# A mixer trunk's three gated merges taken in another order, and a list scheduler that models the port VectorE and GpSimd share

## The chip, the cores and the metric

The kernel runs on one core of a Trainium2 chip. The metric is the device time of one launch in microseconds; a kernel's time is the median of its runs. The engines are called by the profile's names: PE is TensorE's matmul side, DVE is VectorE, ACT is ScalarE, POOL is GpSimd, SP issues the DMAs.

## The reference, cut to what matters

Two layers of a mixer with three parallel branches. Each branch gives a 1024 x 512 result, each result goes through its own projection to 1024 columns, is weighted by a sigmoid gate, and the sum of the three goes through an output projection and is added to the stream.

```python
for l in range(DEPTH):                                   # DEPTH = 2
    h = _rmsnorm(x, norm_g[l])
    (... , gate_logits) = _split_cols(h @ w_in[l])
    y_a = _spatial_gating(...)                           # first branch
    y_b = _mla(...)                                      # second: attention, 8 heads
    y_c = _gla(...)                                      # third: gated linear attention
    gates = jax.nn.sigmoid(gate_logits + b_gate[l]).reshape(bn, s, N_BRANCH, d)
    merged = (gates[:, :, 0] * (y_a @ w_branch[l, 0])
              + gates[:, :, 1] * (y_b @ w_branch[l, 1])
              + gates[:, :, 2] * (y_c @ w_branch[l, 2]))
    x = x + merged @ w_out[l]
```

## The kernel before

Everything is held transposed (columns on partitions) and the sequence of 1024 is cut into two halves h of 512. Numbers are float32, but matmuls take pairs: `pair` (through `split`) makes of each operand a rounded part by an ACT copy and a rest by a DVE subtraction, and each product is three matmuls.

The program is written as segments. A segment has a main list (large products on PE, in steps of about 12 matmuls of 512 columns, here called chunks) and a side list (attention and the like), and `weave` spreads the side steps evenly over the main ones. All instructions go into a `Recorder`, which gives each a cost and a latency by a formula (lines 78 to 121). `Order` then makes one list per engine: `due` counts back from the written order of PE when each instruction is wanted, and `run` plays time forward and lets each free engine take the ready instruction with the earliest due time, within a window (`TUNE`: 30 us ahead on PE, 14 on DVE, ACT and POOL, 22 on SP). It also counts the 94 SBUF buffers of tag `g`, and keeps 6 free for what is due within 4 us. The chip then runs each engine's list in order. In `run` an instruction of one engine never slows one of another.

The stretch that matters is the last third of each layer. `side_att(u, 1)` is the attention of the second half: per block of keys three matmuls, two exponentials on ACT, and two POOL operations on 128 x 512 (a rest and a running sum) in `qk`; per head the transposes of `head_T` (PE into PSUM, an ACT copy and a DVE rest out of it), the row maxima of `mx` on DVE, `negm`. It is woven into this main list:

- `main_merge(u, 2, "yc", ...)`: third branch, both halves, 16 chunks. For each of 8 column tiles n: load and split one weight tile (a DVE subtraction), and per half 12 matmuls and `pe_b`: a DVE operation that multiplies the gate (SBUF) with the product (PSUM), written to `u["m", h, n]`.
- `main_merge(u, 0, "ya", ...)`: first branch, both halves, 16 chunks; `pe_b` also adds to `m` (two SBUF inputs). Its sixteen y tiles are loaded by `load_y` after chunk 12 of the third branch.
- `main_merge(u, 1, "yb", False, True, (0,))`: second branch, half 0, 8 chunks, the last merge: besides multiply and add, `pe_b` makes the rounded part (ACT) and the rest (DVE, two SBUF inputs) for the output projection.
- `main_out(u, (0,))`: its first 12 chunks; each column tile needs two weight tiles split, two chunks and one DVE addition out of PSUM.

The next segment has the rest of the output projection of half 0, then the second branch and the output projection of half 1. `ya` and `yc` wait in DRAM; `yb` of half 0 (8 tiles) is made by the attention of half 0 in the segment ahead and stays in SBUF.

Of the kernel before, what the change touches and what calls it, by code (L numbers as in the profile page):

```python
# [48 lines left out]

class Op:  # L50
    __slots__ = ("i", "eng", "call", "reads", "writes", "cost", "lat", "pred", "succ", "free", "due", "need", "at",
                 "size", "left", "ready", "table")


class Recorder:
# [16 lines left out]
    def add(self, eng, what, fn, a, k):  # L72
        op = Op()
        op.i, op.eng, op.call = len(self.ops), eng, (fn, a, k)
        isap = lambda v: isinstance(v, bass.AP)
        outs = [v for n, v in k.items() if n in ("out", "accum_out") and isap(v)]
        ins = [v for n, v in k.items() if n not in ("out", "accum_out") and isap(v)]
        if a:
            outs.append(a[0])
        op.writes = [v.tensor for v in outs]  # L80
        op.reads = [v.tensor for v in ins]
        op.pred, op.free, op.table = [], [], None
        count = lambda v: int(np.prod(list(v.shape)[1:]))
        n = max(count(v) for v in outs + ins)
        op.size = 0
        if eng == "tensor":
            n = count(k["out"])
            w = k["lhsT"] if what == "matmul" else k["in_"]
            if what == "transpose":
                op.cost = 0.109  # L90
            elif w.dtype == F32R:
                op.cost = 0.0145 + max(n, 256) / 2410.0
            else:
                op.cost = 0.104 if n == 1 else 0.01 + 4 * max(n, 64) / 2400.0
            op.lat = op.cost + 0.3
        elif eng == "vector":
            op.cost = 0.07 + n / 960.0
            if what == "reciprocal":
                op.cost = 0.05 + n / 150.0
            if what == "tensor_tensor_scan":  # L100
                op.cost = 0.1 + n / 480.0
            op.lat = op.cost + 0.25
        elif eng == "scalar":
            op.cost = 0.13 + n / 1200.0
            op.lat = op.cost + 0.25
            f = k.get("func")
            if f is not None:
                op.table = "ln" if f == AF.Ln else "sin" if f == AF.Sin else "" if f in (AF.Copy, AF.Square, AF.Abs,
                                                                                          AF.Relu) else "exp"
        elif eng == "gpsimd":  # L110
            op.cost = {"memset": 0.3, "affine_select": 2.0}.get(what, 0.9 + n / 2000.0)
            op.lat = op.cost + 0.3
        else:
            op.cost = 0.47
            op.size = count(outs[0]) * int(outs[0].shape[0]) * 4
            op.lat = 2.2
        self.ops.append(op)
        return op


class Order:
# [70 lines left out]
    def run(self):  # L192
# [11 lines left out]
        events, order = [], []  # L204
        g = max(self.tags.values(), key=lambda t: t["bufs"])
        relax = 0

        def fits(op, ahead):
            for n in op.need:
# [8 lines left out]
        while done < len(ops):  # L218
            while ptr < len(pe) and pe[ptr].at is not None:
                ptr += 1  # L220
            v = pe[ptr].due if ptr < len(pe) else 1e9
            moved = False
            for e in engines:
                if free[e] > now + 1e-9:
                    continue
                back, pick = [], None
                h = pool[e]
                while h:
                    d, i = heapq.heappop(h)
                    op = ops[i]  # L230
                    if d - v > TUNE["ahead"][e] * (3 if relax else 1):
                        back.append((d, i))
                        break
                    if op.ready <= now + 1e-9 and fits(op, d - v):
                        pick = op
                        break
                    back.append((d, i))
                    if len(back) > 400:
                        break
                for b in back:  # L240
                    heapq.heappush(h, b)
                if pick is None:
                    continue
                op, moved, relax = pick, True, 0
                cost, lat = op.cost, op.lat
                if op.table and op.table != table:
                    table = op.table
                    cost, lat = cost + 1.3, lat + 1.3
                op.at = now
                order.append(op)  # L250
                done += 1
                free[e] = now + cost
                end = now + lat
                if e == "sync":
                    dma = max(dma, now + 1.5) + op.size / 230e3
                    end = dma + 0.7
                for n in op.need:
                    t = self.tags[self.of[n][0]]
                    t["live"] += 1
                    t["next"] += 1  # L260
                heapq.heappush(events, (end, op.i))
                for s in op.succ:
                    s.left -= 1
                    s.ready = max(s.ready, end if s.eng != e or e == "sync" and s.reads[0].name in
                                  {t.name for t in op.writes} else now)
                    if not s.left:
                        heapq.heappush(pool[s.eng], (s.due, s.i))
                heapq.heappush(events, (free[e], -1))
            if moved:
                continue  # L270
            if not events:
                if relax:
                    raise RuntimeError("no order")
                relax = 1
                for n in pool.values():
                    for d, i in n:
                        if ops[i].ready > now:
                            heapq.heappush(events, (ops[i].ready, -1))
                if events:
                    now = heapq.heappop(events)[0]  # L280
                continue
            now, i = heapq.heappop(events)
            while True:
                if i >= 0:
                    op = ops[i]
                    for n in {t.name for t in op.reads + op.writes}:
                        if n in self.left:
                            self.left[n] -= 1
                            if not self.left[n] and n in self.of:
                                self.tags[self.of[n][0]]["live"] -= 1  # L290
                if not events or events[0][0] > now + 1e-9:
                    break
                _, i = heapq.heappop(events)
# [8 lines left out]
class Builder:  # L302
# [846 lines left out]
    def main_merge(self, u, br, key, first, last, hs=(0, 1)):  # L1149
# [3 lines left out]

        def sgl(n):
            for h in hs:
                t = u["sg", h, n] = self.g()
                self.load(t, u.pop(("sgd", h, br * 8 + n)))

        def pe_b(n, h):
            def f():  # L1160
                nc = self.nc
                ps = box.pop("p")
                t = u.pop(("sg", h, n))
                nc.vector.scalar_tensor_tensor(out=t, in0=t, scalar=1.0, in1=ps, op0=ALU.add, op1=ALU.mult)
                if first:
                    u["m", h, n] = t
                    return
                m = u["m", h, n]
                nc.vector.tensor_tensor(out=m, in0=m, in1=t, op=ALU.add)
                if last:  # L1170
                    hi, lo = self.g(dt=F32R), self.g(dt=F32R)
                    nc.scalar.activation(out=hi, in_=m, func=AF.Copy, scale=0.5)
                    nc.vector.scalar_tensor_tensor(out=lo, in0=m, scalar=0.5, in1=hi.bitcast(F32), op0=ALU.mult,
                                                   op1=ALU.subtract)
                    u["mh", h, n] = (hi, lo)
                    del u["m", h, n]
            return f
# [338 lines left out]
    def build(self):  # L1516
# [22 lines left out]
        for i, u in enumerate(units):  # L1539
# [26 lines left out]
            m = []  # L1566
# [8 lines left out]
            a10, a11 = self.side_att(u, 1)  # L1575
            segs.append((m, a00 + a01, 0.0, 0.97))
            mc = self.main_merge(u, 2, "yc", True, False)
            m = mc[:12] + [(0.0, f) for f in y["ya"]] + mc[12:] + self.main_merge(u, 0, "ya", False, False)
            o0 = self.main_out(u, (0,))
            m += self.main_merge(u, 1, "yb", False, True, (0,)) + o0[:12]  # L1580
            segs.append((m, a10 + a11, 0.0, 0.97))
            m = o0[12:] + self.main_merge(u, 1, "yb", False, True, (1,)) + self.main_out(u, (1,))
            sd = []
            if nxt:
                l2 = nxt["l"]
# [97 lines left out]
```

## Time and profile before

| | us |
|---|---|
| median of 3 runs | 2055.52 |
| lowest, highest | 2050.74, 2056.92 |
| the profiled execution | 2053.61 |
| its span, first to last instruction | 2051.8 |
| PE busy in it | 2009.3 (98%) |
| DVE busy | 1535.5 (75%) |
| ACT busy | 1010.4 (49%) |
| POOL busy | 534.6 (26%) |

The profile is of one execution, and a row's time is counted from the start of its span. PE counts as busy from a matmul's start to its modelled end, and matmuls overlap. All instructions were recorded through one helper and carry its line, L1603, so they are told apart by engine, operation and tile: `mm` is the PSUM tile of a main product, `sc`, `tr` and `av` those of the side work, `g` any SBUF tile of the general pool.

### The profile page before, as it was taken

How to read it: one execution, taken by the hardware profiler on the slowest of the kernel's cores; microseconds unless marked ns; L12 is line 12 of the kernel's file. 1: busy time of each engine (PE TensorE's matmuls, PEld its weight loads, DVE VectorE, ACT ScalarE, POOL GpSimd, SP SyncE). 2: the span in 40 equal slices, each digit the busy share in tenths (PEclk: the TensorE clock that was granted, in tenths of full speed). 3: DMA queues.
4: the chain of work that ended last, by engine and by line, in shares of the span. 5: the costliest groups of instructions: out<-in, count | busy, mean ns of one | idle time of the engine just before them, and what ended most of it. 6: DMA issues, size and time to landing. Idle time of an engine off the chain costs nothing. (4 is left out here: it accounts for less than half of the span.)

```text
span 2051.8 us, 29332 instructions
## 1 busy us (share of the span) xinstructions
PE 2009.3 (98%) x9864; PEld 1650.9 (80%) x9864; DVE 1535.5 (75%) x2779; ACT 1010.4 (49%) x1969; POOL 534.6 (26%) x460
## 2 busy tenths in 40 slices
PE   6999999999999999999999999999999999999999
PEld 5887778888888887777889877788888888877777
DVE  7576657867878868997855756588689788699873
ACT  6465344554566634454434653354445665444441
POOL 1110111001124456665002001100011334666630
PEclk9999999999999999999999999999999999999999
DMA  6261233443533855425742512345246338544252
GB/s 244 89 227 67 83 127 131 139 164 130 188 118 97 268 185 152 136 84 190 250 146 103 200 67 94 113 144 185 98 139 199 115 114 277 175 125 141 93 205 88
DMA packets 216327, 302.14 MB, mean 147 GB/s; under 512 B 63176, under 2 KB 91880, under 8 KB 216176
## 3 DMA queue, kind: packets, MB, share of 16 engines
q1 hardware_dynamic: 216176, 300.26, 44.0%
q8 instruction: 78, 1.28, 0.3%
q14 instruction: 73, 0.60, 0.1%
HBM read 207.76 MB, written 92.43 MB: 146 GB/s over the span
## 5 line engine op out<-in xcount | busy, mean ns | idle before, releaser
L1603 PE MATMUL mm<-g,g 128*128 128x512 f32 (+1 forms) x6480 | 1589.8, 393 | 3.8 <-ACT g L1603 2.8
L1603 PEld LDWEIGHTS mm<-g,g 128*128 128x128 f32 x6480 | 1201.2, 189 | 249.9 <-ACT g L1603 6.2
L1603 DVE TENSOR_TENSOR g<-g,g 128x512 fp32r<-128x512 f32 (+4 forms) x1053 | 747.3, 742 | 153.9 <-ACT g L1603 143.8
L1603 ACT CAST g<-g 128x512 fp32r<-128x512 f32 (+3 forms) x704 | 401.6, 601 | 238.3 <-DVE g L1603 177.3
L1603 POOL TENSOR_TENSOR g<-g,g 128x256 f32<-128x256 f32 (+5 forms) x352 | 415.9, 1202 | 386.3 <-ACT g L1603 267.6
L1603 ACT ACTIVATE g<-sc 128x512 f32<-128x512 f32 (+5 forms) x432 | 199.8, 510 | 234.5 <-PE sc L1603 213.9
L1603 PE MATMUL sc<-g,g 64*64 64x64 f32 (+8 forms) x1632 | 263.4, 299 | 0.0
L1603 PEld LDWEIGHTS sc<-g,g 64*64 64x64 f32 (+4 forms) x1632 | 202.9, 172 | 37.8 <-issue 4.7
L1603 DVE TENSOR_TENSOR g<-mm,g 128x512 f32<-128x512 f32 (+1 forms) x176 | 117.3, 673 | 123.9 <-PE mm L1603 81.8
L1603 ACT COPY g<-mm 128x512 f32<-128x512 f32 (+1 forms) x168 | 97.0, 580 | 219.2 <-PE mm L1603 210.9
L1603 PE MATMUL av<-g,g 128*128 128x512 f32 (+3 forms) x672 | 186.0, 365 | 2.9 <-POOL g L1603 2.8
L1603 ACT ACTIVATE g<-g 128x512 f32<-128x512 f32 (+3 forms) x225 | 129.5, 590 | 106.9 <-DVE g L1603 89.0
L1603 PEld LDWEIGHTS av<-g,g 128*128 128x128 f32 x672 | 122.8, 190 | 23.2 <-POOL g L1603 6.5
L1603 DVE SCALAR_TENSOR_TENSOR g<-g,g 128x512 f32<-128x512 f32 (+3 forms) x185 | 126.4, 695 | 5.8 <-ACT g L1603 3.8
L1603 DVE TENSOR_REDUCE mx<-tr 128x1 f32<-128x512 f32 (+1 forms) x192 | 104.4, 569 | 17.6 <-PE tr L1603 16.7
L1603 PE MATMUL tr<-g,g 128*64 128x128 f32 (+5 forms) x416 | 102.8, 345 | 9.8 <-DVE mx L1603 7.6
L1603 DVE SCALAR_TENSOR_TENSOR g<-g,mm 128x512 f32<-128x512 f32 x112 | 76.2, 681 | 42.2 <-PE mm L1603 27.6
L1603 POOL TENSOR_TENSOR qr<-qv,mhalf 128x8 f32<-128x8 f32 x16 | 29.1, 1817 | 282.4 <-DVE qv L1603 282.4
L1603 PEld LDWEIGHTS tr<-g,g 115*128 115x128 f32 (+2 forms) x416 | 62.4, 175 | 34.6 <-DVE mx L1603 16.5
L1603 PE MATMUL tr<-ident,g 128*96 128x128 f32 (+2 forms) x480 | 77.2, 273 | 7.4 <-DVE g L1603 7.4
L1603 PEld LDWEIGHTS tr<-ident,g 128*96 128x96 f32 (+2 forms) x480 | 57.5, 129 | 24.1 <-DVE g L1603 7.9
L1603 POOL TENSOR_SCALAR_AFFINE_SELECT g<-g 128x512 f32<-128x512 f32 x16 | 10.5, 656 | 251.2 <-ACT g L1603 251.0
(119 smaller groups left out, 882.3 us busy)
## 6 DMA issues: line engine op xcount, KB each, us to landing
g<-wT SPq DMA_DIRECT2D x176, 256.0 KB
sg<-g SPq DMA_DIRECT2D x96, 256.0 KB
g<-sg SPq DMA_DIRECT2D x96, 256.0 KB
g<-wbr SPq DMA_DIRECT2D x64, 256.0 KB
g<-wo SPq DMA_DIRECT2D x64, 256.0 KB
g<-kd SPq DMA_DIRECT2D x48, 192.0 KB
g<-xT SPq DMA_DIRECT2D x32, 256.0 KB
hd<-g SPq DMA_DIRECT2D x32, 256.0 KB
```

The lines of the kernel that those rows point to most:

```text
L1603: ins = real[op.i] = fn(*a, **k)
```

## The change

The merges are written in another order. The third branch's two chunks of column tile n (half 0, half 1) are followed by the second branch's half 0 of the same tile, for n = 0 to 7 (24 chunks; the loads of `ya` stand after chunk 20). Then comes the first branch, both halves (16 chunks), which is now the last merge of half 0: there `pe_b` makes the pair for the output projection, for half 0 alone (`last` is now a tuple of halves). The 12 chunks of the output projection follow as before. Half 1 of the second branch stays in the next segment and stays the last merge of that half. Gate tiles get the branch into their key, since two branches are now open at once.

In the scheduler, an instruction has a flag `lock`: a DVE instruction with two SBUF inputs among `in0`, `in1`, `in_`, and a POOL instruction with at least one. When `run` places one, it adds to its cost and latency the time until the other engine's last such instruction ends. The cost formula of POOL is new: 0.22 + n/600 us in place of 0.9 + n/2000, and 0.8 for up to 64 elements.

```diff
--- before.py
+++ after.py
@@ -49,7 +49,7 @@
 
 class Op:
     __slots__ = ("i", "eng", "call", "reads", "writes", "cost", "lat", "pred", "succ", "free", "due", "need", "at",
-                 "size", "left", "ready", "table")
+                 "size", "left", "ready", "table", "lock")
 
 
 class Recorder:
@@ -80,6 +80,8 @@
         op.writes = [v.tensor for v in outs]
         op.reads = [v.tensor for v in ins]
         op.pred, op.free, op.table = [], [], None
+        near = sum(v.space == bass.MemoryType.SB for n_, v in k.items() if n_ in ("in0", "in1", "in_") and isap(v))
+        op.lock = eng == "vector" and near > 1 or eng == "gpsimd" and near > 0
         count = lambda v: int(np.prod(list(v.shape)[1:]))
         n = max(count(v) for v in outs + ins)
         op.size = 0
@@ -108,7 +110,7 @@
                 op.table = "ln" if f == AF.Ln else "sin" if f == AF.Sin else "" if f in (AF.Copy, AF.Square, AF.Abs,
                                                                                           AF.Relu) else "exp"
         elif eng == "gpsimd":
-            op.cost = {"memset": 0.3, "affine_select": 2.0}.get(what, 0.9 + n / 2000.0)
+            op.cost = {"memset": 0.3, "affine_select": 2.0}.get(what, 0.22 + n / 600.0 if n > 64 else 0.8)
             op.lat = op.cost + 0.3
         else:
             op.cost = 0.47
@@ -204,6 +206,7 @@
         events, order = [], []
         g = max(self.tags.values(), key=lambda t: t["bufs"])
         relax = 0
+        port = {"vector": 0.0, "gpsimd": 0.0}
 
         def fits(op, ahead):
             for n in op.need:
@@ -246,6 +249,10 @@
                 if op.table and op.table != table:
                     table = op.table
                     cost, lat = cost + 1.3, lat + 1.3
+                if op.lock:
+                    wait = max(0.0, port["gpsimd" if e == "vector" else "vector"] - now)
+                    cost, lat = cost + wait, lat + wait
+                    port[e] = now + cost
                 op.at = now
                 order.append(op)
                 done += 1
@@ -1153,21 +1160,21 @@
 
         def sgl(n):
             for h in hs:
-                t = u["sg", h, n] = self.g()
+                t = u["sg", br, h, n] = self.g()
                 self.load(t, u.pop(("sgd", h, br * 8 + n)))
 
         def pe_b(n, h):
             def f():
                 nc = self.nc
                 ps = box.pop("p")
-                t = u.pop(("sg", h, n))
+                t = u.pop(("sg", br, h, n))
                 nc.vector.scalar_tensor_tensor(out=t, in0=t, scalar=1.0, in1=ps, op0=ALU.add, op1=ALU.mult)
                 if first:
                     u["m", h, n] = t
                     return
                 m = u["m", h, n]
                 nc.vector.tensor_tensor(out=m, in0=m, in1=t, op=ALU.add)
-                if last:
+                if last and h in last:
                     hi, lo = self.g(dt=F32R), self.g(dt=F32R)
                     nc.scalar.activation(out=hi, in_=m, func=AF.Copy, scale=0.5)
                     nc.vector.scalar_tensor_tensor(out=lo, in0=m, scalar=0.5, in1=hi.bitcast(F32), op0=ALU.mult,
@@ -1575,11 +1582,13 @@
             a10, a11 = self.side_att(u, 1)
             segs.append((m, a00 + a01, 0.0, 0.97))
             mc = self.main_merge(u, 2, "yc", True, False)
-            m = mc[:12] + [(0.0, f) for f in y["ya"]] + mc[12:] + self.main_merge(u, 0, "ya", False, False)
+            mb = self.main_merge(u, 1, "yb", False, False, (0,))
+            m = sum((mc[2 * n:2 * n + 2] + mb[n:n + 1] for n in range(8)), [])
+            m = m[:20] + [(0.0, f) for f in y["ya"]] + m[20:] + self.main_merge(u, 0, "ya", False, (0,))
             o0 = self.main_out(u, (0,))
-            m += self.main_merge(u, 1, "yb", False, True, (0,)) + o0[:12]
+            m += o0[:12]
             segs.append((m, a10 + a11, 0.0, 0.97))
-            m = o0[12:] + self.main_merge(u, 1, "yb", False, True, (1,)) + self.main_out(u, (1,))
+            m = o0[12:] + self.main_merge(u, 1, "yb", False, (1,), (1,)) + self.main_out(u, (1,))
             sd = []
             if nxt:
                 l2 = nxt["l"]
```

## Rows read from the trace of the kernel before

**Rows 1.** The page, span and busy times: engine, busy us, share of the span, instructions.

```profile
span 2051.8 us, 29332 instructions
...
PE 2009.3 (98%) x9864; PEld 1650.9 (80%) x9864; DVE 1535.5 (75%) x2779; ACT 1010.4 (49%) x1969; POOL 534.6 (26%) x460
```

**Rows 2.** Busy time by stretch: window, length, then per engine; the granted clock, DMA.

```profile
690.00:770.00 80.00, 79.31 (x382) 64.95 (x381) 58.78 (x93) 34.53 (x69) 39.49 (x35) 1.00 0.70 218
770.00:840.00 70.00, 68.42 (x327) 55.62 (x326) 61.52 (x83) 31.93 (x67) 45.82 (x38) 1.00 0.42 128
840.00:890.00 50.00, 44.05 (x207) 35.61 (x206) 49.01 (x66) 25.37 (x49) 27.15 (x21) 0.97 0.45 139
890.00:970.00 80.00, 78.38 (x362) 63.55 (x361) 67.08 (x96) 41.05 (x84) 47.17 (x39) 1.00 0.43 142
...
1855.00:1905.00 50.00, 45.35 (x205) 36.50 (x204) 48.02 (x65) 24.85 (x49) 26.45 (x21) 0.93 0.45 139
...
sum 560.00, PE 540.88 PEld 439.39 DVE 468.33 ACT 262.93 POOL 319.38; mean PE 67.61 PEld 54.92 DVE 58.54 ACT 32.87 POOL 39.92
```

**Rows 3.** Waits of PE, 840 to 890: who waited for whom, total us, times, longest.

```profile
PE tr L1603 <- DVE g L1603: 4.4, 1, 4.4
PE tr L1603 <- DVE mx L1603: 1.6, 1, 1.6
```

**Rows 4.** Timeline, 850 to 900: start, length, instruction, idle before it in brackets.

```profile
852.14 2.98 POOL L1603 TENSOR_TENSOR g<-g,g 128x512 fp32r<-128x512 f32 x2 [0.26 <-ACT g L1603]
...
852.49 1.50 DVE L1603 TENSOR_TENSOR g<-g,g 128x512 f32<-128x512 f32 x1
...
854.02 1.65 DVE L1603 SCALAR_TENSOR_TENSOR g<-g,g 128x512 f32<-128x512 f32 x1
...
855.59 1.01 DVE L1603 TENSOR_REDUCE mx<-tr 128x1 f32<-128x512 f32 x2
...
856.33 0.77 PE L1603 MATMUL tr<-g,g 115*128 115x512 f32 x2 [1.58 <-DVE mx L1603]
...
870.62 0.60 PE L1603 MATMUL tr<-ident,g 128*96 128x128 f32 x4
...
879.72 1.09 PE L1603 MATMUL tr<-ident,g 128*96 128x128 f32 x4 [4.37 <-DVE g L1603]
```

**Rows 5.** DVE groups, 770 to 840: count, busy us, mean ns, idle before and releaser.

```profile
L1603 DVE TENSOR_TENSOR g<-g,g 128x512 f32<-128x512 f32 x14 | 16.3, 1164 | 0.3
L1603 DVE TENSOR_TENSOR g<-g,g 128x512 fp32r<-128x512 f32 x12 | 12.9, 1089 | 1.2 <-ACT g L1603 1.0 <-DMA g<-sg 0.2
L1603 DVE SCALAR_TENSOR_TENSOR g<-g,mm 128x512 f32<-128x512 f32 x15 | 10.2, 682 | 6.4 <-PE mm L1603 6.3
```

**Rows 6.** Two of the stretches, instructions on PSUM tiles mm alone (main matmuls).

```profile
770.00:840.00 70.00, 46.19 (x180) 33.31 (x180) 10.17 (x15) 0.00 (x0) 1.00 0.42 128
840.00:890.00 50.00, 27.73 (x109) 20.02 (x108) 6.07 (x9) 0.00 (x0) 0.97 0.45 139
```

**Rows 7.** Timeline of DVE, 676 to 716: the second branch's last tile, then the merge.

```profile
704.94 3.39 DVE L1603 RECIPROCAL g<-tr 128x128 f32<-128x128 f32 x4 [1.43 <-PE tr L1603]
...
713.22 0.68 DVE L1603 SCALAR_TENSOR_TENSOR g<-g,g 128x512 f32<-128x512 f32 x1
...
714.75 0.67 DVE L1603 SCALAR_TENSOR_TENSOR g<-g,mm 128x512 f32<-128x512 f32 x1
```

**Rows 8.** Busy time in the first 50 us of the span.

```profile
0.00:50.00 50.00, 34.39 (x153) 29.54 (x154) 39.76 (x97) 33.33 (x73) 6.68 (x12) 1.00 0.70 250
```

**Rows 9.** Groups of the whole run, POOL: count, busy us, mean ns, idle before it.

```profile
L1603 POOL TENSOR_TENSOR g<-g,g 128x512 fp32r<-128x512 f32 x96 | 133.3, 1392 | 266.2 <-ACT g L1603 166.7 <-issue 42.5 <-PE mm L1603 25.3
...
L1603 POOL TENSOR_TENSOR qr<-qv,mhalf 128x8 f32<-128x8 f32 x16 | 29.1, 1817 | 282.4 <-DVE qv L1603 282.4
```

**Rows 10.** Tile negm: count, shortest, median and longest ns of its instructions.

```profile
L1603 DVE TENSOR_SCALAR negm<-negm x16: 169/170/1219, 720.0 to 1940.8; 128x4 f32<-128x4 f32 x16
```

**Rows 11.** Timeline of the DMA queue, 736 to 754: loads of the first branch.

```profile
737.95 12.39 SPq L1603 DMA_DIRECT2D g<-ya  x16
```

## The prediction

> **What bounds the kernel now.** I read the page first: PE is busy for 2009.3 of 2051.8 us [rows 1], so the time is PE's work and all that can be won or lost is PE's idle time, 42.5 us, and the time in which its clock is low. Then the busy time by stretch, to find the idle time. The reader is to look at PE's busy time against the length of each stretch, and at DVE's beside it. In the eight stretches in which the second half's attention and the merges run (four in each layer, 560 us in all) PE is idle for 560 - 540.88 = 19.1 us [rows 2]. Half of that lies in two short ones: 840 to 890 in the first layer (50 - 44.05 = 5.95 us) and 1855 to 1905 in the second (4.65 us), and there DVE is busy 49.01 and 48.02 of 50 us [rows 2]. The granted clock falls there as well, to a mean of 0.97 and 0.93; between the levels 2.4 and 1.2 GHz that costs 50 x 0.03 = 1.5 and 50 x 0.07 = 3.5 us [rows 2]. So the two places cost 5.95 + 1.5 + 4.65 + 3.5 = 15.6 us together.
>
> Next, who PE waits for there: DVE, once for 4.4 us and once for 1.6 us, and nobody else [rows 3]. The timeline shows why. Two additions and rests with two SBUF inputs take 1.50 and 1.65 us while POOL runs, the row maxima queue behind them, and PE's next matmuls begin 1.58 us late [rows 4]. The same form of PE instruction takes 0.60 us at 870.62 and 1.09 us at 879.72, after the 4.37 us wait: that is the low clock [rows 4].
>
> Last, why DVE is full just there. Its operations with two SBUF inputs on 128 x 512 take 1164 and 1089 ns on average from 770 to 840, and the one that reads PSUM and one SBUF tile, of the same size, 682 ns [rows 5]. So sharing with POOL adds some 400 to 480 ns to each of the first kind.
>
> **The interleaved merges.** No instruction is added or removed; they move. DVE operations per chunk, counted from the code (those with two SBUF inputs in brackets): third branch 1.5 (0.5), first 2.5 (1.5), second with the pair 4 (3), output projection 1.5 (1). Before, the order is 16 chunks of 1.5, 16 of 2.5, 8 of 4 and 12 of 1.5, 114 in all. After, it is 24 chunks of 2 (1), 16 of 3 (2) and 12 of 1.5, again 114. The peak of 4 becomes 3 and is twice as long. What that means is read off the stretches:
>
> - The stretch 770 to 840 is mostly first branch. Its 180 main matmuls are 15 chunks [rows 6], on which DVE spends 61.52 / 15 = 4.10 us per chunk, side work included, and PE 68.42 / 15 = 4.56 [rows 2]. DVE keeps up.
> - The stretch 840 to 890 is second branch: 109 matmuls, 9.1 chunks [rows 6]; DVE 49.01 / 9.1 = 5.4 us per chunk, PE (44.05 - 1.5) / 9.1 = 4.7 [rows 2]. DVE is short by 0.7 us per chunk, 6.4 us in all, which is what PE lost there.
> - After, the 16 chunks of 3 have half an operation more than the present first branch, with two SBUF inputs: 4.10 + 0.5 x 1.13 = 4.66 us of DVE for 4.56 of PE, short by 0.10 x 16 = 1.6 us. If the added operation takes the 682 ns of an undisturbed one, the figure is 4.44 and nothing is lost. If it takes 1.65 us, as the slow one in the timeline [rows 4], it is 4.92, short by 5.8 us; with more blocking of its neighbours I call it 7. I take 2 per layer, near the mean row.
> - The first 24 chunks: 690 to 770 holds the third branch, DVE busy 58.78 of 80 us [rows 2]. Half an operation more per chunk, on some 18 chunks, is 18 x 0.5 x 1.1 = 10 us, which fits into the 21 us that DVE idles. No cost; if the cover were gone, PE would pay up to 10 us.
>
> So of 15.6 us some 2 x 2 = 4 come back as a longer, lower overload, and about 11.6 are won. The clock's share goes with the wait: in the other rows without a wait of several us it is 1.00 [rows 2].
>
> **What moves on the queues.** On SP the second branch's 8 weight tiles and 8 gate tiles of half 0 come ahead of the 16 loads of `ya` and of the first branch's 8 and 16; `ya` goes from behind chunk 12 to behind chunk 20. The DMA share in the stretch where they then fall is 0.42, less than the 0.70 where they are now [rows 2], so the queue itself costs nothing. POOL and ACT issue no DMA. The output projection gains slack: the pair of its last column tile is now made two chunks ahead of its use, and not one.
>
> **A new dependency.** The second branch's half 0 must now be complete at the third chunk, not at the 33rd. Its last tile's reciprocals begin at 704.94 and its last multiplication ends at 713.90; the first merge's DVE operation is at 714.75 [rows 7]. A copy and a subtraction are still missing then (about 1.4 us at 0.68 each), and two chunks at 4 to 5 us lie in between. It is ready in time; the cover is those two chunks and the third branch's next ones, and without it PE waits up to 4 us.
>
> **The scheduler's model.** It takes no blocked time away; it lets the lists put PE's next instructions where their inputs are ready. It reshuffles all engines in the whole program. The trace shows no run under it, so I bound it by PE's idle time that lies outside both the eight stretches and the start: 42.5 - 19.1, less the 50 - 34.4 = 15.6 us of the first 50 [rows 8], is 7.8 us. Either way it can hardly be more than that: -8 to +8, and I take 0. The cost formula of POOL matters less: it gives 1.07 us for 512 elements where the mean is 1.39 (the model of the port adds waits to that), and 0.8 us for the 8-wide power where the row says 1.82 [rows 9]; the old one gave 0.9, so the error grows by 0.1.
>
> **The sum.** Against the profiled execution, 2053.61 us (1.8 us around its span): 2053.6 - 15.6 + 4 = 2042. That execution lies 1.9 us below the median of the runs shown, so I add half of this: 2043 us.
>
> **The rivals.**
> 1. DVE stays the bound. The 400 to 480 ns that a two-input operation loses beside POOL [rows 5] stay as they are, and spreading the work only spreads the wait. For it: the stretch 770 to 840 already has DVE at 61.52 of 70 us [rows 2], and the excess on its 26 two-input operations is 14 x 0.48 + 12 x 0.41 = 11.6 us [rows 5]. Against it: PE idled only 70 - 68.42 = 1.58 us there [rows 2]. At 7 us per layer, 14 of the 15.6 come back: 2052. Chance 0.2. The Trainium skill, "SBUF — State Buffer", section "Who interferes with whom", says that whichever of the two starts first holds the shared pair for its whole instruction and the other blocks fully, and that this is so for a DVE instruction with two SBUF inputs against a POOL one that reads SBUF. The durations above agree. It also names one-input DVE forms such as `tensor_scalar` as takers of the pair, which the change's `lock` leaves out, and the trace bears that out: the 128 x 4 one on `negm` takes 170 ns in the median and 1219 at worst [rows 10]. By that rule the new lists stay partly blind.
> 2. Buffers run out (slower). The third branch's 16 tiles are held until chunk 24, not 16, together with the 8 of the second, while the 16 of `ya` must come in. For it: the pool has 94 buffers for all this and the attention. Against it: after chunk 24 all 24 come free at once, and PE has attention work in the list. It takes place at chunk 25 if the loads of `ya` can't start before chunk 24 ends: the 16 issues take 12.39 us [rows 11], paid in each layer: 2042 + 2 x 12.4 = 2067. It decides from 20 us on, that is with 13 of the 16 loads late in both layers (0.77 us each). Chance 0.1.
> 3. The model does more than I give it and PE never waits in the eight stretches: 2053.6 - 19.1 - 5 = 2029.5. Chance 0.07.
> 4. The change doesn't do what it says: the lists come out with new waits elsewhere (the +8 above): 2050. Chance 0.08.
>
> **How the numbers follow.** The forecast, 2043, has 0.55 and a range of its own of 2036 to 2049. A measurement of this kernel can tell 0.3%, 6.2 us, from no change, so faster is below 2049.4 and slower above 2061.7. Faster: 0.55, rival 3, and half of rival 4, whose 2050 is next to the bound: 0.66. Slower: rival 2, 0.1. The rest, 0.24, is within. The range of 8 in 10 leaves out rival 3 and rival 2 and goes from 2042 - 8 = 2034 to 2042 + 14 = 2056: 7 per layer at worst from the longer overload, or 8 from the lists with part of it.
>
> **What would show it.** Right: the wait of 4.4 us on DVE is gone in both layers, the granted clock is 1.00 in the second half's attention, DVE is busy 90 to 96% evenly, PE idles 8 to 10 us in the eight stretches in place of 19.1. Wrong: PE waits on `mx` or `tr` spread over the 16 chunks of the first branch (rival 1), or waits for loads of `ya`, or with DVE idle, near the 24th chunk (rival 2). The step most likely to be wrong is the 2 us per layer.

## The result, and the profile after

The changed kernel takes 2029.28 us (median of 4 runs, 2028.83 to 2029.9) beside 2056.22 for the one before; the ratio is 0.9876, 95% interval 0.9865 to 0.9888. The forecast was 2043 with a range of 2034 to 2056, so it was wrong: some 27 us were won where 12 were expected. The two profiled executions are 24.3 us apart (2053.61 and 2029.29), since that of before lies 2.6 us below this median.

The page of after, span, busy times by engine (share, instructions), and the granted clock in 40 slices:

```profile
span 2027.6 us, 29291 instructions
...
PE 2000.4 (99%) x9864; PEld 1648.0 (81%) x9864; DVE 1543.7 (76%) x2779; ACT 1011.8 (50%) x1969; POOL 542.2 (27%) x460
...
PEclk9999999999999999999999999999999999999999
```

Each of these engines runs as many instructions as before [rows 1]. The span is 24.2 us shorter: PE idles 27.2 us and not 42.5 (15.3 less) and is busy 8.9 us less. Most of the latter is low clock that is gone: the mean granted clock of the execution is 1.00 and was 0.996, which is some 8 us of 2051.8.

Busy time by stretch in the second half's attention, both layers (window, length, PE, PE's weight loads, DVE, ACT, POOL, then granted clock, DMA share, GB/s), which answers to [rows 2]; the stretches are cut a little otherwise, since the work has moved:

```profile
690.00:770.00 80.00, 79.71 (x379) 64.40 (x378) 70.41 (x102) 37.68 (x75) 40.58 (x34) 1.00 0.63 192
770.00:850.00 80.00, 79.73 (x387) 65.41 (x386) 70.17 (x95) 39.45 (x80) 51.57 (x42) 1.00 0.57 176
850.00:910.00 60.00, 58.90 (x280) 47.81 (x279) 58.79 (x83) 31.29 (x63) 38.63 (x30) 1.00 0.31 103
910.00:960.00 50.00, 49.83 (x229) 40.91 (x229) 39.01 (x62) 25.83 (x53) 31.52 (x26) 1.00 0.59 185
...
sum 540.00, PE 536.31 PEld 437.06 DVE 475.51 ACT 265.69 POOL 324.87; mean PE 67.04 PEld 54.63 DVE 59.44 ACT 33.21 POOL 40.61
```

PE idles 540 - 536.31 = 3.7 us in the eight stretches, where it idled 19.1 [rows 2]. Outside them nothing has changed: 27.2 - 3.7 = 23.5 us now, 42.5 - 19.1 = 23.4 before. Yet DVE is as full as ever: 58.79 of 60 us from 850 to 910. It is not that DVE got room; PE no longer stands still when DVE is late.

The DVE groups of after from 770 to 850 (count, busy us, mean ns, idle before) beside [rows 5]:

```profile
L1612 DVE TENSOR_TENSOR g<-g,g 128x512 fp32r<-128x512 f32 x14 | 15.1, 1082 | 0.3 <-ACT g L1612 0.2
L1612 DVE TENSOR_TENSOR g<-g,g 128x512 f32<-128x512 f32 x10 | 11.1, 1108 | 0.1
L1612 DVE SCALAR_TENSOR_TENSOR g<-g,mm 128x512 f32<-128x512 f32 x16 | 10.8, 680 | 8.4 <-PE mm L1612 8.3
```

The delays beside POOL are still there, 1082 and 1108 ns against 680.

And how it looks in order of time, after, from 850 on (start, length, instruction, idle before it), beside [rows 4]:

```profile
850.30 2.98 POOL L1612 TENSOR_TENSOR g<-g,g 128x512 fp32r<-128x512 f32 x2 [0.78 <-ACT g L1612]
...
850.68 1.46 DVE L1612 TENSOR_TENSOR g<-g,g 128x512 f32<-128x512 f32 x1
...
850.93 2.02 PE L1612 MATMUL mm<-g,g 128*128 128x512 f32 x8
...
852.06 0.68 DVE L1612 SCALAR_TENSOR_TENSOR g<-g,mm 128x512 f32<-128x512 f32 x1
...
852.66 1.01 DVE L1612 TENSOR_REDUCE mx<-tr 128x1 f32<-128x512 f32 x2
...
853.39 0.77 PE L1612 MATMUL tr<-g,g 115*128 115x512 f32 x2 [0.45 <-DVE mx L1612]
```

The same scene as at 852 before: two POOL operations, a DVE addition held up to 1.46 us, row maxima behind it. But only one held-up operation stands in front of the maxima, and PE waits 0.45 us in place of 1.58.

Where the time was won, from the PE records: the moment at which PE has streamed the same number of columns, after minus before, at moments of before.

| moment before, us | 50 | 700 | 850 | 950 | 1100 | 1700 | 1850 | 1950 | 2000 |
|---|---|---|---|---|---|---|---|---|---|
| after minus before, us | +1.1 | -0.5 | -2.3 | -10.8 | -11.7 | -13.5 | -15.2 | -22.9 | -24.3 |

Some 10 us in each layer's second-half attention, the rest in small steps. Counted in the same way, 840 to 890 gives 5.4 us and 1855 to 1905 gives 5.7, the two places that the prediction names.

### The profile page after: what moved, and what is told of

Same layout as the page of the kernel before. It is cut to its first block, busy times and chain, and to the rows that moved or that the text cites. A ratio compares the mean times of both kernels' runs of the same rounds, so it can differ in the third digit from the quotient of the medians.

```text
span 2027.6 us, 29291 instructions
## 1 busy us (share of the span) xinstructions
PE 2000.4 (99%) x9864; PEld 1648.0 (81%) x9864; DVE 1543.7 (76%) x2779; ACT 1011.8 (50%) x1969; POOL 542.2 (27%) x460
## 4 chain that ended last, share of the span: by engine, by line
PE 91%; DVE 6%; POOL 1%; ACT 1%; issue 1%; DMA 0%; SPq 0%; DVEq 0%; POOLq 0%; ACTq 0%
PE mm L1612 68%; PE sc L1612 10%; PE tr L1612 7%; PE av L1612 6%; DVE g L1612 5%; POOL g L1612 1%; DVE mx L1612 1%; ACT g L1612 1%; DMA g<-xT 0%; POOL hr L1612 0%; DVE negm L1612 0%; SPq L1612 0%; DVE hv L1612 0%; DVEq L1612 0%; POOLq L1612 0%
## 5 line engine op out<-in xcount | busy, mean ns | idle before, releaser
L1612 DVE TENSOR_TENSOR g<-g,g 128x512 fp32r<-128x512 f32 (+5 forms) x1053 | 755.8, 750 | 137.4 <-ACT g L1612 122.9
```

The source lines that it names most:

```text
L1612: ins = real[op.i] = fn(*a, **k)
```

## The experiments

Three edits make up the change: the order of the merges (O), the port in the scheduler (P), and the POOL costs (C). Each could be had alone. In the tables below, "before" is the median of the kernel before, measured together with the run.

**Each part alone.** O without P and C, with both left at what they were:

```diff
-                if op.lock:
-                    wait = max(0.0, port["gpsimd" if e == "vector" else "vector"] - now)
-                    cost, lat = cost + wait, lat + wait
-                    port[e] = now + cost
-... 0.22 + n / 600.0 if n > 64 else 0.8)
+... 0.9 + n / 2000.0)
```

> The new order of the merges alone, with the old scheduler (no port, old POOL costs). Theory A (the lower peak of DVE work does it): it keeps most of the 27 us, 2032 to 2038, and PE's wait of 4.4 us on DVE in the second half's attention is gone. Theory B (the lists do it, because they know when DVE is held up): only the part of the peak is won, 2042 to 2048, and short waits of PE on DVE of 0.6 to 2 us stay in all of that stretch, with some low clock.

Measured 2043.28 us beside 2054.15, ratio 0.9942 (0.9924 to 0.9959), as theory B has it. The first layer's bad stretch, to be held against the third row of [rows 2], and PE's wait for the row maxima from 690 to 970 (total us, times, longest):

```profile
840.00:890.00 50.00, 46.78 (x219) 36.66 (x218) 49.50 (x70) 23.52 (x46) 28.46 (x22) 1.00 0.40 117
```

```profile
PE tr L1608 <- DVE mx L1608: 2.5, 4, 1.5
```

PE idles 3.2 us in place of 5.95 and the clock is up, so the long wait is gone and short ones of up to 1.5 us stay.

The next three leave the merges in their old order:

```diff
-            mb = self.main_merge(u, 1, "yb", False, False, (0,))
-            m = sum((mc[2 * n:2 * n + 2] + mb[n:n + 1] for n in range(8)), [])
-            m = m[:20] + ... + m[20:] + self.main_merge(u, 0, "ya", False, (0,))
+            m = mc[:12] + ... + mc[12:] + self.main_merge(u, 0, "ya", False, ())
             o0 = self.main_out(u, (0,))
-            m += o0[:12]
+            m += self.main_merge(u, 1, "yb", False, (0,), (0,)) + o0[:12]
```

with P and C:

> The new scheduler (port and POOL costs) with the old order of the merges. Theory A: DVE is still short by 0.7 us per chunk over the 9 chunks of the second branch, so at most 3 us are won, 2050 to 2056. Theory B: PE takes other ready work while DVE is late, most of the idle time goes, 2034 to 2042.

with P alone (the old costs put back as above):

> The port in the scheduler alone: old POOL costs, old order of the merges. Theory A: within 3 us of before. Theory B: like the port and the costs together, within 2 us of that run, since the costs differ by 0.1 to 0.4 us only.

and with C alone (the four lines of the port taken out):

> The new POOL costs alone: no port in the scheduler, old order of the merges. Both theories: no change beyond 4 us from 2055, since neither the DVE work nor what the lists know of its delays changes. A gain of 8 us or more would make the costs a third cause.

Then the change with one of its parts taken out, O and P with the old costs, and O and C without the port:

> The change with the old POOL costs. Theory C1 (the old costs already held a mean of the port's waits, and with the port they are counted twice; that hurts in either order): 5 to 7 us slower than the change, as it was with the old order, 2034 to 2037. Theory C2 (the interleaved order leaves DVE room enough that the error does no harm): within 2 us of the change, 2028 to 2031.

> The change without the port: new order of the merges, new POOL costs. Theory B (the port in the scheduler does it, and shorter POOL costs alone make it more wrong): 2043 to 2050, no better than the order of the merges alone. Theory A (the order does it, the port is a detail): 2029 to 2035.

| | old order, us | new order (O), us |
|---|---|---|
| no port, old costs | 2054 to 2056 (before) | 2043.28 |
| no port, new costs (C) | 2060.16, ratio 1.0031 (1.002 to 1.0042) | 2048.87, ratio 0.9973 (0.9963 to 0.9983) |
| port (P), old costs | 2037.92, ratio 0.992 (0.9902 to 0.9937) | 2040.95, ratio 0.9937 (0.9922 to 0.9952) |
| port and new costs | 2031.82, ratio 0.9889 (0.9875 to 0.9904) | 2029.28 (the change) |

Theory A, that the lower peak of DVE work does it, is out: the order alone brings 11 us, and the port with its costs brings 22 without touching the order. Under the port the order is worth 2.5 us with the new costs by the medians (the intervals of the two ratios overlap), and nothing (3 us the other way) with the old ones. The costs are no detail: without the port they lose 6 us in either order, and with it they win 6 and 12; C1 expected 5 to 7 for the last. They were written for a scheduler that adds the waits itself. Two more expectations were missed: P alone was to lie within 2 us of P with C and lies 6 above it, and C alone was to change nothing beyond 4 us. In each of the four pairs the port wins, but with the new order and the old costs it wins only 2.3 us, less than a small step in a cost moves a time (below).

The busy time by stretch in the old order with port and new costs, to be held against the third row and the last but one of [rows 2]:

```profile
840.00:890.00 50.00, 48.12 (x232) 39.81 (x231) 49.72 (x67) 28.41 (x57) 39.01 (x29) 1.00 0.52 154
1855.00:1905.00 50.00, 48.13 (x232) 39.41 (x232) 49.68 (x69) 28.75 (x58) 34.95 (x26) 1.00 0.40 120
```

DVE has not got less to do in these 50 us (49.72, and 49.01 before), but PE issues 232 instructions in place of 207 and 205, and POOL, which works for the attention here, is busy 39.0 and not 27.2 us in the first row. Of the 25 more in the first row 10 are main products (119, and 109 [rows 6]), the rest is attention: the lists put work there whose inputs are ready. (The second row holds somewhat later work than the row of before, since this kernel is some 13 us ahead by then.) This is so with port and costs together. With the port alone the stretch from 840 to 890 stays nearly as it was, PE busy 45.72 us, DVE 42.69, clock 0.97, and most of what that run wins lies elsewhere.

**Is it the when, or only a mean delay?** P replaced by a fixed 0.25 us on the same operations, old order, new costs:

```diff
                 if op.lock:
-                    wait = max(0.0, port["gpsimd" if e == "vector" else "vector"] - now)
+                    wait = 0.25
                     cost, lat = cost + wait, lat + wait
-                    port[e] = now + cost
```

> Old order of the merges, new POOL costs; in place of the port, every two-input DVE operation and every POOL operation that reads SBUF gets 0.25 us more in the scheduler's run. That is the mean that the port adds to such an operation in the second half's attention, given without knowing when. Theory B1 (it matters to know when the port is taken): the gain of port and costs together, 22 us, is mostly lost, 2045 to 2060. Theory B2 (the scheduler only thought VectorE and GpSimd too fast on average): it stays, 2030 to 2038.

Measured 2045.65 us beside 2054.69, ratio 0.9959 (0.9944 to 0.9974). The fixed delay wins 14.5 us over C alone, but stays 13.8 behind the port. That doesn't show that the moments are worth the other half. In the bad stretches the fixed delay does as well as the port: PE is busy 49.44 of the 50 us from 840 to 890 and again from 1855 to 1905, at a clock of 1.00 (48.12 and 1.00 with the port in the first). What is missing is lost elsewhere. From 50 to 690 us PE idles 4.1 us, and 1.1 in the run with the port, and it waits for ACT:

```profile
PE mm L1609 <- ACT g L1609: 10.0, 11, 2.2
```

That wait is 2.2 us in the run with the port, at the start of the kernel. The 0.25 us were the mean of the second half's attention, where POOL is busy more than half of the time [rows 2]; from 50 to 690 it is busy 103 of 640 us, so there the same 0.25 is likely too much. Other values, or one for each stretch, were not tried, and what the moments alone are worth stays open.

**Is it PE's list or DVE's?** The scheduler plays twice. The first run, with the port, gives the lists of some engines; a second one without it must follow these and makes the others. PE's list kept:

```diff
+        keep = {}
+        for op in Order(self.nc.ops, outside).run():
+            keep.setdefault(op.eng, []).append(op.i)
         known = Order(self.nc.ops, outside)
-        for op in known.run():
+        for op in known.run(False, {e: keep[e] for e in ('tensor',)}):
```

> Old order of the merges, new POOL costs. Two plannings: PE's list is that of the run with the port (2031.8 us as a whole), the lists of VectorE, GpSimd, ScalarE and SyncE are from a run without it that has to follow this PE list. Theory D1 (the gain lies in where PE's instructions stand): 2031 to 2038. Theory D2 (it lies in the order of the DVE and POOL lists): near the run with the new costs and no port, 2052 to 2060.

and the lists of DVE, POOL and ACT kept, `('vector', 'gpsimd', 'scalar')` in the last line:

> The reverse: the lists of VectorE, GpSimd and ScalarE from the run with the port, PE's and SyncE's from a run without it that has to follow them. Theory D1: most of the gain is lost, 2045 to 2060. Theory D2: it stays, 2031 to 2038.

Measured 2056.16 (ratio 1.0008, 0.9999 to 1.0017) and 2054.66 us (1.0, 0.9991 to 1.0009) beside 2054.78. Both theories fall: with either half of the good lists nothing is left of the 22 us. (Against the new costs without the port, 2060.16, some 4 and 5.5 us are left of 28.) PE's waits in the two (total us, times, longest), PE's list kept first:

```profile
PE tr L1619 <- DVE g L1619: 26.3, 7, 11.9
PE tr L1619 <- DVE mx L1619: 5.1, 10, 0.7
PE av L1619 <- DVE g L1619: 2.7, 2, 1.4
PE av L1619 <- POOL g L1619: 2.7, 4, 1.2
```

and with the other lists kept:

```profile
PE tr L1619 <- DVE g L1619: 16.9, 6, 12.3
PE av L1619 <- POOL g L1619: 9.1, 13, 1.7
PE mm L1619 <- DVE g L1619: 3.7, 9, 0.7
```

(About 15 us of the first line is the start of the kernel in all of them.) In the first PE's good list waits for DVE, and the bad stretch is there as before: PE is busy 44.90 us from 840 to 890 at a clock of 0.93. In the second a PE list made without the port waits for POOL; there PE is busy 48.37 us in that stretch, and what it wins is lost right behind, 75.61 of the 80 us from 890 to 970. The gain came only where all lists were made in one playing of time that has the delays in it, so that they meet.

**How near must the model be, and is it a lucky draw?** The change with POOL's wide costs times a factor, for instance

```diff
-... 0.22 + n / 600.0 if n > 64 else 0.8)
+... 0.95 * (0.22 + n / 600.0) if n > 64 else 0.8)
```

> The change with the POOL costs of wide operations 5% lower, a step much smaller than any error of the model. If the 27 us are what the port's model is worth, 2027 to 2032. If the lists fall well or badly by chance, and the change's 2029 is a lucky draw, it is off by several us: 2034 to 2045.

> The change with POOL's wide costs at 0.85. Theory E1 (with the port modelled, a POOL cost below the real one is better, since a wait of the two engines on each other is put on both): 2022 to 2027. Theory E2 (each list is a draw; the level of the cost means nothing): anywhere from 2025 to 2045.

> The same at 0.75. Theory E1 has an end: here POOL is planned at 0.81 us for 512 elements where the trace has 1.29, so PE should wait for POOL: 2026 to 2036. Theory E2: anywhere from 2025 to 2045.

> The same at 1.05. Theory E1: a few us above the change, 2030 to 2036, on the way to the 2041 of the fitted costs. Theory E2: anywhere from 2025 to 2045.

> The change with POOL's wide costs at 1.18: 1.27, 1.02 and 0.76 us for 512, 384 and 256 elements, as measured; narrow powers and the select stay at 0.8 and 2.0. If the level of the wide costs is what makes the fitted costs worse, 2037 to 2043, as with them. If it is the narrow powers and the select, 2030 to 2034, near the 2031 of 1.05.

The kernel before with its costs times 0.95, to see a draw without the port:

> The kernel before with its POOL costs at 0.95, no port: how far a step without a meaning moves a list that knows nothing of the port. If lists fall by chance within some 5 us, 2050 to 2060. If a kernel without the port can fall as well as the change does, below 2040, the port's share is not shown.

The costs fitted to the trace, narrow operations and the select too (`0.2 + n / 467.0 if n > 64 else 0.5 + n * 0.163`, select 0.65 in place of 2.0), and these with one-input operations added to the flag (`near > 1 or near and what in ("tensor_scalar", "tensor_copy")`):

> The change with POOL costs fitted to the undisturbed durations of the trace: 0.2 + n/467 us (0.75, 1.02 and 1.30 for 256, 384 and 512), 0.5 + 0.163 n for the narrow powers (1.8 us at 8), 0.65 for the select, in place of 1.07 at 512, 0.8 and 2.0. If what the lists know is what counts, a nearer model gives a little more: 2024 to 2029. If PE's order is as good as it gets with the present costs, within 2 us of 2029.

> As the run with fitted POOL costs, and one-input DVE operations (tensor_scalar, tensor_copy out of SBUF) take the port as well. The trace has the small one on negm at 170 ns in the median and 1222 ns at worst. Few of them meet a POOL operation, so within 2 us of the run with fitted costs; if they block PE's chain of the row maxima, 2 to 4 us faster than it.

And 0.95 with the old order:

> The port with POOL costs at 0.95 on the old order of the merges, beside 2024.4 with the new order. If the order is worth the same under the port whatever the costs, 2025 to 2029 (2.5 us more, as at 1.00). If it is worth what it is without the port, 2034 to 2037 (11 us more).

| kernel, all with the port | planned us for 512 | us | ratio |
|---|---|---|---|
| factor 0.75 | 0.81 | 2040.28 | 0.9927 (0.9913 to 0.9942) |
| 0.85 | 0.91 | 2032.23 | 0.9888 (0.9872 to 0.9905) |
| 0.95 | 1.02 | 2024.37 | 0.9854 (0.9837 to 0.987) |
| 0.95, old order | 1.02 | 2026.73 | 0.9855 (0.9838 to 0.9871) |
| 1.00, the change | 1.07 | 2029.28 | 0.9876 (0.9865 to 0.9888) |
| 1.05 | 1.13 | 2031.07 | 0.988 (0.9865 to 0.9895) |
| 1.18, the measured wide costs | 1.27 | 2031.51 | 0.9878 (0.9863 to 0.9892) |
| all fitted | 1.30 | 2041.46 | 0.9934 (0.9919 to 0.995) |
| all fitted, one-input ones too | 1.30 | 2040.73 | 0.9931 (0.9915 to 0.9948) |
| no port, before at 0.95 | 1.10 | 2061.8 | 1.0033 (1.0022 to 1.0044) |

The port is not a lucky draw. The twelve kernels that have it (from one playing of time) lie between 2024 and 2041, the six without it (before and the fixed delay among them) between 2043 and 2062. Within each group a step of a tenth or less in the factor moves the time by up to 8 us. With factors between 0.85 and 1.18 it is 2024 to 2032. Theory E1, that costs below the real ones are better, fell: 0.85 gave 2032.23 and not 2022 to 2027, and 0.75 lies above its 2036. At 0.75 POOL is planned too fast and PE waits for it, 6.0 us on `av`, and some 7 us more than at the start for DVE:

```profile
PE tr L1612 <- DVE g L1612: 21.3, 5, 11.7
PE av L1612 <- POOL g L1612: 6.0, 4, 1.6
```

while at 0.95 nothing is left but the start and crumbs:

```profile
PE tr L1612 <- DVE g L1612: 15.6, 3, 12.5
PE mm L1612 <- ACT g L1612: 2.2, 1, 2.2
PE tr L1612 <- DVE mx L1612: 0.8, 2, 0.4
PE av L1612 <- POOL g L1612: 0.6, 2, 0.3
```

This kernel, 2024.37 us, is faster than the change. In the old order 0.95 gives 2026.73: the order is worth 2.4 us under the port by the medians, as at 1.00, and nothing by the ratios (0.9854 and 0.9855). Either way it is the smaller of the two possibilities expected, and not 11 us.

My expectation that nearer costs give more was wrong. The measured wide costs (1.18) lose 2 us to the change by the medians and nothing by the ratios; what costs the other 10 is in the fitted narrow powers and the select. Why these few operations matter is not shown. The page of the fitted kernel says where it shows, not why:

```profile
span 2039.7 us, 29308 instructions
...
PE 2009.9 (99%) x9864; PEld 1653.5 (81%) x9864; DVE 1545.0 (76%) x2779; ACT 1011.0 (50%) x1969; POOL 540.0 (26%) x460
```

PE idles 29.8 us there, 2.6 more than after; but it is busy 9.5 us longer with the same instructions, at a mean granted clock of 0.997. Some 6 us of that are low clock; the rest is not explained. Why the best factor lies below the measured durations stays open. Adding the one-input operations changes nothing that can be told (0.9931 beside 0.9934).

## Why the prediction was wrong

- **What bounds the kernel: right.** PE's idle time and its low clock. PE's idle time shrank by 15.3 us and its busy time by 8.9. Of the gain some 11 us lie in the two places named, and 16, two thirds, with the 60 and 45 us behind them.
- **The interleaved merges: right, as far as it goes.** 11.6 us were worked out for the order with nothing for the scheduler, that is 2043 us, and the order alone gave 2043.28, 10.9 us less than the kernel before. The DVE load of the 16 chunks was put at 4.66 us each; from 850 to 910 of the changed kernel DVE is busy 58.79 us with 150 main matmuls, 12.5 chunks, which is 4.70. The 2 us per layer that were to come back, which I called the step most likely to be wrong, are near what PE still idles with the order alone, 3.2 us from 840 to 890.
- **The scheduler's model: the step that failed.** It was given 0, bounded by 8 us either way. With its costs it is worth 14 us on top of the order (2.3 with the old costs) and 22 on its own. The bound was wrong in its place: I took PE's idle time outside the eight stretches as all that the model could reach. Just that did not move (23.4 and 23.5 us). The idle time inside I counted as the order's, though of its 19.1 us the order was credited with the 10.6 of the two places alone, and the other 8.5 with nobody; 3.7 are left of all. Inside, I read "DVE is short by 0.7 us per chunk" as a fact of the work; it was a fact of how the lists mixed main and side work in those 50 us. With port and costs, DVE is just as full and PE does 25 instructions more [rows 2]. The 15.6 us of the two places could thus be had in two ways: counted by PE's columns as in the table above, the order alone wins 9.9 there, port and costs in the old order 16.5, and the fixed delay, which knows no moments, 13.7. Of the other 9 us of the change some 5 are idle time elsewhere in the stretches and some 4 low clock.
- **"The cost formula of POOL matters less": wrong.** Without the port it loses 6 us, with it it wins 6 to 12. An error of 0.1 to 0.4 us per operation was too small to matter only in a sum of busy times; in the playing of time it changes the lists. Which meetings of instructions cost or save the time was not traced.
- **Rival 1, the delays only spread: wrong as a rival, right as a statement.** The delays are as long as before (1082 and 1108 ns), and cost PE next to nothing: it idles 3.7 us in the eight stretches. That the lists stay blind for one-input operations, as the rule of the Trainium skill, "SBUF — State Buffer", section "Who interferes with whom", would have it, costs nothing that the runs can tell (2040.73 with them in the flag, 2041.46 without, both with the fitted costs).
- **Rival 2, buffers: did not come.** The 16 loads of `ya` went out in one row of 13.81 us, which ended some 14 us before the chunks that read them, and no wait of PE on a load shows in that attention:

```profile
779.07 13.81 SPq L1612 DMA_DIRECT2D g<-ya  x16
```

- **Rival 3 happened.** "The model does more than I give it and PE never waits", 2029.5 us, at a chance of 0.07. The mechanism is the one that came. That the number fits to 0.2 us is luck: PE still idles 3.7 us there, and the busy time fell by 8.9 us and not by the 5 of clock in its sum, and the two errors cancel. It should have had the larger part.
- **The new dependency on `yb` and the queues: right,** no wait was seen.
- **The clock: right.** It went with the waits: 1.00 in all eight stretches after.

## What to carry to other kernels

Where lists for in-order engines are planned ahead, an engine that is full is not by itself a bound: ask whether the others have ready work and whether the plan knows the delay. Model a delay between the two engines that cause it, and then take the averages of it out of the costs: the port alone stayed 6 us or more behind both, and the costs alone lost 6. A mean delay did as well in the stretch that it was taken from, and lost elsewhere. Plan the lists of all engines in one playing of time, and try a few values of each cost, since steps of 5% moved this kernel by 2 to 6 us.

## What was not expected of the hardware

The clock does not fall after every wait of the same length. At the border of the layers PE waits 0.98 us for DVE before and 0.99 us after, behind the same instructions; the granted clock is 0.85 in those 10 us before, and 1.00 after (windows as above, then PE in order of time; before first):

```profile
1050.00:1060.00 10.00, 9.02 (x40) 7.53 (x39) 4.46 (x8) 5.61 (x11) 1.40 (x1) 0.85 0.00 0
...
1055.65 1.02 PE L1603 MATMUL tr<-ones,g 128*128 128x1 f32 x8 [0.98 <-DVE g L1603]
...
1057.59 3.07 PE L1603 MATMUL mm<-g,g 128*128 128x512 f32 x7
```

```profile
1040.00:1050.00 10.00, 8.95 (x43) 6.93 (x42) 4.94 (x9) 5.79 (x12) 1.40 (x1) 1.00 0.00 1
...
1045.17 1.02 PE L1612 MATMUL tr<-ones,g 128*128 128x1 f32 x8 [0.99 <-DVE g L1612]
...
1046.84 1.76 PE L1612 MATMUL mm<-g,g 128*128 128x512 f32 x7
```

The same seven matmuls behind the wait take 3.07 us and 1.76. So a wait of 1 us costs 1 us or 2.5 here (0.15 x 10 = 1.5 us of clock), and two kernels with the same wait can differ by 1.5 us at one such place. How much of the spread between the kernels with the port this makes was not counted. What decides it is not shown.
